# Rotating an 8192 x 8192 matrix: the first macro tile's outputs, TensorE's eight reduced to two

## The chip, the cores and the metric

The kernel runs on one core of one Trainium2 chip. The metric is device time in microseconds (us) of one execution; three runs of the kernel before gave 1258.72, 1258.84 and 1259.64 us, median 1258.84.

A core has several engines that run their own instruction streams: TensorE (PE in the profile), VectorE (DVE), ScalarE (ACT), GpSimd (POOL) and SyncE (SP). SP and ACT also start the DMAs, the transfers between HBM and the on-chip memory (SBUF), each into a queue of its own; 16 DMA engines serve both queues. PSUM is TensorE's output memory.

## The reference

```python
def setup_inputs():
    return {"x": np.random.randn(8192, 8192).astype(np.float32), "k": 1}

def reference(x, k):
    return np.rot90(x, k)
```

With k = 1 the output is `out[8191 - c, r] = x[r, c]`: a transpose with the column order reversed. 268 MB are read and 268 MB are written; there is no arithmetic.

## The kernel before

**Tiles.** The input is cut into 16 macro tiles of 1024 rows x 4096 columns, `kk` = 0 to 15. A macro tile is loaded in eight row blocks (`t` = 0 to 7) of 128 rows x 4096 columns, 2 MB each; load `m = 8 kk + t`. It gives eight outputs (`j` = 0 to 7), each 512 output rows x 1024 output columns, 2 MB; output `n = 8 kk + j`. An output needs its 512-column part, a chunk, of all eight loads. So store `n` can only start when the macro tile's last load has landed.

**Buffers.** Five buffers of 16 KB per partition: two for landing loads, three for outputs. During the first macro tile all five land loads (`load_buf`: loads 0 to 4 go to buffers 0 to 4, loads 5 to 7 to 0 to 2, load 8 to 4, later ones alternate between 0 and 1). Output buffers are given by `START` in macro tile 0 (buffers 3, 2, 4, 3, 2, 4, 3, 2) and by `TURN` later. `room_for` waits until the buffer's last store has landed or, for a buffer's first output, until its last load has been taken out. Between the landing buffers and the outputs lies `ring`, with 63 slots of one chunk. Load `m` writes its chunks into the slots that output `n = m - 8` has just emptied (`slot` runs the other way round in every second macro tile). VectorE therefore turns load `m` only after output `m - 8` has been read out of the ring.

**Two ways to make an output.** `by_pe(kk)` lists the outputs of a macro tile that TensorE makes. For those, VectorE copies the chunk into the ring with its columns reversed, TensorE transposes its 128 x 128 blocks into two PSUM halves, and ScalarE copies the halves to the output buffer (three copies for an output). All others are marked `moved`. For these VectorE writes the chunk with a 32 x 32 block transpose (`STREAM_TRANSPOSE`), and the 32 x 32 blocks are then brought to their places by 16 copies of 32 partitions x 1024 elements: the first 3 by VectorE, the next 8 by GpSimd, the last 5 by ScalarE (`BY_DVE`, `BY_POOL`). In the middle macro tiles `BY_PE = [0, 4]`. Before the change macro tile 0 makes all eight outputs by TensorE, and so does the last one.

The last load of a macro tile has no slot for its last chunk (63 slots for 64 chunks): VectorE reverses that chunk inside the landing buffer, and TensorE transposes it, the "corner", into PSUM. The corner comes ahead of the last part of output 0 on TensorE.

**Order of the work.** Every engine follows a written-out order, with semaphore waits between engines:

- VectorE (`by_vector`) goes through the loads. For load `m`, with `n = m - 8`: if output `n` is moved, it makes its three copies for it; then it waits for the landing, then for GpSimd's and its own copies of output `n` (`s_pool`, `s_dve`), or for TensorE's transposes of it (`s_half`), and then turns the load.
- GpSimd (`by_gpsimd`) goes through the moved outputs: `room_for`, the load that completes the output, seven copies, a wait for ScalarE's copies (`s_act`), the eighth.
- TensorE (`by_tensor`) goes through the outputs of `by_pe`.
- ScalarE (`by_scalar`) issues loads 1, 3 and 5 and half of loads 6 to 9, then goes through all outputs: its five copies, or the three PSUM evictions, then the store's DMA. Ahead of the store of a moved output it waits until VectorE has turned the first chunk of load `n + 8`, which tells it that VectorE's and GpSimd's copies are done.
- SyncE (`by_sync`) issues the other loads, each when its landing buffer has been taken out.

VectorE's and TensorE's programs for macro tiles 2 to 13 and GpSimd's for 1 to 12 run in a hardware loop; the rest is written out.

All operations are issued by one helper, L104 of the profile, so the groups are told apart by engine and tile. L391 is the DMA of `load`.

Of the kernel before, what the change touches and what calls it, by code (L numbers as in the profile page):

```python
# [173 lines left out]
def kernel(tc: tile.TileContext, x: bass.AP, k: bass.AP, out: bass.AP):  # L174
# [7 lines left out]
    KK = len(macros)  # L182
# [11 lines left out]
    outs = [(*o, [(j, g * P) for j in reversed(o[2]) for g in range(G)]) for o in outs]  # L194

    def by_pe(kk):
        if kk in (0, KK - 1):
            return list(range(J))
        return BY_PE if kk < KK - 2 else [*range(0, J, 2), J - 1]

    def in_quadrants(kk, j):
        return j not in by_pe(kk)
# [127 lines left out]
    for m in range(n_load):  # L330
        kk, t = divmod(m, T)
        here = by_pe(kk)
        rest = [j for j in range(J) if j not in here]
        if kk == KK - 1:
            got = [here] if t < T - 1 else [here[:wide], here[wide:-1], here[-1:]]
        elif t < T - 1:
            got = [here, rest]
        else:
            inner = [j for j in here if 0 < j < J - 1]
            got = [here[:1], [j for j in rest if j < J - 1], [J - 1], inner]  # L340
        got = [part for js in got for part in split(js)]
        pieces[m] = got
        for js in got:
            done += 1
            for j in js:
                rev[m, j] = done
# [289 lines left out]
```

## Time and profile before

| | before |
|---|---|
| median of three runs | 1258.84 us |
| the profiled execution, its own time | 1259.08 us |
| its span, first to last instruction | 1257.8 us |
| mean DMA rate over the span | 427 GB/s |
| DVE busy | 793.8 us (63%) |
| POOL busy | 744.0 us (59%) |
| ACT busy | 599.6 us (48%) |
| PE busy | 302.9 us (24%) |

A page of the profile is read from the top: the busy time of each engine, the same in 40 slices of the span (31.4 us each) with the rate of the DMAs beneath, the DMA queues, the chain of work that ended last, and the groups of instructions. A group's line gives engine, operation, what is written and read, shape and count; then the busy time and mean of one; then the idle time of the engine ahead of them and what ended it. A line of the timeline begins with its start and the time it covers, both in us from the span's start; "x3" are three instructions merged, and the bracket is the idle time ahead and what ended it.

### The profile page before, as it was taken

The page shows a single profiled execution, that of the slowest core. Times are in us where ns is not written, and L with a number is a line of the kernel's source. Part 1 is how long each engine was busy: PE and PEld are TensorE (multiplying, and loading weights), DVE is VectorE, ACT ScalarE, POOL GpSimd, SP SyncE. Part 2 cuts the span into 40 slices and gives each one's busy share as a digit, 9 for nine tenths or more (in the row PEclk, how much of TensorE's full clock was granted, in tenths as well). Part 3 has the DMA queues.
Part 4 walks back from the last instruction along what each step waited for, and adds up shares of the span by engine and source line. Part 5 has one row for each costly group of instructions (what it writes and reads, how often), then busy time and mean ns, then how long its engine had stood idle before and what let it go on. Part 6 is the DMA issues. An engine that isn't in the chain of part 4 may idle for free.

```text
span 1257.8 us, 6012 instructions
## 1 busy us (share of the span) xinstructions
PE 302.9 (24%) x1556; PEld 264.8 (21%) x1556; DVE 793.8 (63%) x535; ACT 599.6 (48%) x556; POOL 744.0 (59%) x654
## 2 busy tenths in 40 slices
PE   1555013130131301313022130221302213024273
PEld 0454012130121301212012120121202212024273
DVE  2544866668666676666867667676677766764410
ACT  0334364463644636446364453645535455355364
POOL 0001966668666686666956668576685766965500
PEclk9987556555555555555556555565555556555597
DMA  9999999999999999999999999999999999999999
GB/s 400 420 430 429 429 429 429 429 431 430 430 430 429 430 428 430 428 430 430 430 430 429 431 428 431 428 430 428 430 430 429 430 429 431 427 423 428 427 428 381
DMA packets 36946, 537.09 MB, mean 427 GB/s; under 512 B 4160, under 2 KB 4160, under 8 KB 4160
## 3 DMA queue, kind: packets, MB, share of 16 engines
q10 hardware_dynamic: 19184, 278.93, 52.2%
q1 hardware_dynamic: 17744, 257.96, 48.0%
q8 instruction: 7, 0.11, 0.0%
q14 instruction: 11, 0.09, 0.0%
HBM read 268.44 MB, written 268.44 MB: 427 GB/s over the span
## 4 chain that ended last, share of the span: by engine, by line
DMA 71%; DVE 14%; ACT 4%; POOL 4%; issue 3%; PE 2%; ACTq 0%; DVEq 0%; SPq 0%; POOLq 0%
DMA buf<-in_x_dram 57%; DMA out_dram<-buf 14%; DVE ring L104 14%; ACT buf L104 4%; POOL buf L104 4%; PE ps L104 2%; ACTq L104 0%; DVE buf L104 0%; DVEq L101 0%; SPq L391 0%; DVEq L145 0%; POOLq L101 0%; SPq L311 0%; POOLq L151 0%; SPq L419 0%
## 5 line engine op out<-in xcount | busy, mean ns | idle before, releaser
L104 POOL COPY buf<-ring 32x1024 f32<-32x1024 f32 (+1 forms) x648 | 743.3, 1147 | 440.4 <-DMA out_dram<-buf 244.2
L104 ACT COPY buf<-ring 32x1024 f32<-32x1024 f32 (+1 forms) x405 | 414.8, 1024 | 324.2 <-DVE ring L104 292.5
L104 PE MATMUL ps<-head,ring 128*128 128x128 f32 x1496 | 290.7, 372 | 889.4 <-ACT buf L104 535.8
L104 PEld LDWEIGHTS ps<-head,ring 128*128 128x128 f32 x1496 | 255.3, 197 | 921.5 <-ACT buf L104 548.7
L104 DVE COPY ring<-buf 128x1024 f32<-128x1024 f32 (+5 forms) x152 | 157.7, 1044 | 415.6 <-DMA buf<-in_x_dram 320.1
L104 DVE STREAM_TRANSPOSE ring<-buf 128x3072 f32<-128x3072 f32 (+2 forms) x125 | 358.0, 2872 | 0.0
L104 ACT COPY buf<-ps 128x2048 f32<-128x2048 f32 (+4 forms) x149 | 183.3, 1278 | 313.6 <-DMA out_dram<-buf 149.3
L104 DVE COPY buf<-ring 32x1024 f32<-32x1024 f32 (+1 forms) x243 | 289.5, 1192 | 2.2
L104 PE MATMUL ps<-head,buf 128*128 128x128 f32 x60 | 15.2, 401 | 46.3 <-DVE buf L104 46.3
L104 PEld LDWEIGHTS ps<-head,buf 128*128 128x128 f32 x60 | 9.7, 199 | 52.0 <-issue 44.6
L104 DVE COPY buf<-buf 128x512 f32<-128x512 f32 x15 | 5.8, 387 | 0.0
L104 ACT ACT_TABLE_LOAD x1 | 1.3, 1283 | 3.4 <-PEq L419 3.4
L104 POOL MEMSET head<- 128x128 f32 x1 | 0.2, 204 | 2.9 <-POOLq L419 2.9
L104 POOL TENSOR_SCALAR_AFFINE_SELECT head<-head 128x128 f32<-128x128 f32 x1 | 0.3, 293 | 0.2 <-POOL head L104 0.2
L617 POOL MEMSET const-float32-0.0<- 128x1 f32 x1 | 0.1, 98 | 0.2 <-issue 0.2
L104 ACT COPY head<-head 128x1 f32<-128x1 f32 x1 | 0.2, 191 | 0.0
L617 POOL MEMSET const-bfloat16-1.0<- 128x1 bf16 x1 | 0.1, 100 | 0.0
L617 POOL MEMSET const-uint8-127<- 128x1 uint8 x1 | 0.1, 100 | 0.0
L617 POOL MEMSET const-float32-1.0<- 128x1 f32 x1 | 0.1, 98 | 0.0
## 6 DMA issues: line engine op xcount, KB each, us to landing
out_dram<-buf ACTq DMA_DIRECT2D x128, 2048.0 KB, 15.8
buf<-in_x_dram SPq DMA_DIRECT2D x121, 2048.0 KB, 15.0
buf<-in_x_dram ACTq DMA_DIRECT2D x3, 2048.0 KB, 16.9
buf<-in_x_dram SPq DMA_DIRECT2D x4, 1024.0 KB, 16.1
buf<-in_x_dram ACTq DMA_DIRECT2D x4, 1024.0 KB, 16.4
```

Source lines behind the costliest of these rows:

```text
L104: i = getattr(e, self.name)(*self.args, **kwargs)
L617: nc = _bacc.Bacc("TRN2", target_bir_lowering=False, num_devices=1)
```

## The change

In macro tile 0 TensorE makes outputs 0 and 4, as in the middle macro tiles. Outputs 1, 2, 3, 5, 6 and 7 are moved.

```diff
     def by_pe(kk):
-        if kk in (0, KK - 1):
+        if kk == KK - 1:
             return list(range(J))
         return BY_PE if kk < KK - 2 else [*range(0, J, 2), J - 1]
```

`by_pe` is read wherever a program is written: by `moved`, by the pieces in which VectorE turns a load, and by the loops of all engines over the outputs. So for loads 0 to 7 VectorE copies two chunks of eight and transposes six. While it turns loads 8 to 15 it adds three copies for each of six outputs. GpSimd gets eight copies for each of six outputs, and ScalarE five copies in the place of three evictions. TensorE keeps the two outputs and the corner. Buffers, DMAs and their order on each queue are as before.

## The prediction

> **What bounds the kernel now.** I read the page's slices first, then the chain, then the groups, then the timeline of the first 154 us, where the change lies.
>
> ```profile
> DMA  9999999999999999999999999999999999999999
> GB/s 400 420 430 429 429 429 429 429 431 430 430 430 429 430 428 430 428 430 430 430 430 429 431 428 431 428 430 428 430 430 429 430 429 431 427 423 428 427 428 381
> ...
> DMA 71%; DVE 14%; ACT 4%; POOL 4%; issue 3%; PE 2%; ACTq 0%; DVEq 0%; SPq 0%; POOLq 0%
> ```
>
> The DMA engines are busy in every slice, at some 430 GB/s: one 2 MB transfer (2.097 MB) takes 4.88 us of all 16 engines. No engine is above 63%. Engine work costs nothing by itself; it costs only when both DMA queues run dry. So the question is whether the change opens a gap in the transfers, and the place is the start, where the first store needs eight loads. Slice 0 holds the start-up, slice 1 a dip that I return to. The timeline of the start:
>
> ```profile
> 32.60 4.50 DVE L104 COPY ring<-buf 128x4096 f32<-128x4096 f32 x2 [5.26 <-DMA buf<-in_x_dram]
> ...
> 42.31 0.43 DVE L104 COPY ring<-buf 128x512 f32<-128x512 f32 x1 [2.56 <-DMA buf<-in_x_dram]
> 42.77 0.43 DVE L104 COPY buf<-buf 128x512 f32<-128x512 f32 x1
> ...
> 45.87 0.64 ACTq L104 DMA_DIRECT2D out_dram<-buf  x1
> ...
> 53.27 0.58 ACTq L104 DMA_DIRECT2D out_dram<-buf  x1
> ...
> 59.03 0.55 ACTq L104 DMA_DIRECT2D out_dram<-buf  x1
> ```
>
> Loads 4 and 5 land together at 32.6, load 7 at 42.3; the corner is ready at 43.2 and store 0 is issued at 45.87, 2.66 later. Stores 1 and 2 follow before store 0 is through, so that the store queue is two deep from here on. What a moved output costs is seen where macro tile 1 begins:
>
> ```profile
> 122.42 1.53 DVE L104 COPY ring<-buf 128x1024 f32<-128x1024 f32 x1 [5.97 <-DMA buf<-in_x_dram]
> 123.88 3.36 DVE L104 STREAM_TRANSPOSE ring<-buf 128x3072 f32<-128x3072 f32 x1
> 127.17 4.33 DVE L104 COPY buf<-ring 32x1024 f32<-32x1024 f32 x3
> 132.43 0.69 DVE L104 COPY ring<-buf 128x1024 f32<-128x1024 f32 x1 [0.93 <-POOL buf L104]
> ...
> 133.16 0.55 ACTq L104 DMA_DIRECT2D out_dram<-buf  x1
> 133.75 5.25 ACT L104 COPY buf<-ring 32x1024 f32<-32x1024 f32 x5 [6.35 <-DVE ring L104]
> 136.34 4.34 DVE L104 COPY buf<-ring 32x1024 f32<-32x1024 f32 x3
> 142.68 0.69 DVE L104 COPY ring<-buf 128x1024 f32<-128x1024 f32 x1 [2.00 <-POOL buf L104]
> ...
> 143.40 0.55 ACTq L104 DMA_DIRECT2D out_dram<-buf  x1
> ```
>
> VectorE waits for POOL ahead of each turn, and stores come every 10.25 us (133.16, 143.40, 153.65). A load and a store take the DMA 2 x 4.88 = 9.76 us. Three moved outputs in a row are thus 0.5 us each slower than the DMA; macro tile 1 lives off the stores queued before it. In macro tile 0 nothing is queued yet.
>
> **The change part by part.**
>
> *Turning loads 0 to 7.* Removed: copies of 128x4096, 2.29 us a load. Added: a 128x1024 copy and a 128x3072 transpose; from 132.43 to 136.34 that is 3.91 us. Loads land every 4.88 us, but loads 0 to 5 in pairs, so VectorE falls behind: load 4 from 32.6, 5 from 36.5, 6 from 40.4, 7 from 44.3 (landed 42.3). In macro tile 1's last load the corner was ready 3.55 us after the first chunk was begun (112.57 to 116.12). So the corner is at 47.85, not 43.2. Loads 8 to 10 need loads 4 to 6 turned, by 44.3 at the latest; the loads ahead of them run until about 52. Hidden; uncovered, it would cost the 4.65 us.
>
> *Store 0.* Corner + 2.66 = 50.5, 4.6 us later. Load 9 runs to 52.2 and load 10 is behind it on SP's queue, so nothing idles. Load 10 and store 0 are through at 52.2 + 9.76 = 62.0 (packet records of before: 62.2 and 62.8); I take 62.2. ScalarE's first eviction also starts some 3 us later, because it issues half of load 9 first, which needs load 5; its cover is the corner.
>
> *Output 1 to 3.* Removed: TensorE's 32 transposes and ScalarE's 3.9 us of evictions each, both off the path. Added on ScalarE: 5.25 us, begun as soon as the store before is issued, 5 us before POOL needs it. Added on VectorE: 4.34 us, inside POOL's time. Added on POOL: 8 copies, 10.2 us. POOL can begin when the corner is transposed (buffer 2): 47.85 + 1.1 (four of the eight transposes that took 1.98 us) + 0.1 = 49.1. Done at 59.3. Queued behind it are VectorE's turn of load 9 and, by the first chunk of that, store 1, 0.7 us later: 60.0 against 53.27. Then every 10.25 us: store 2 at 70.3, store 3 at 80.5. Load 11 (after load 9 turned) goes out at 63.3, load 12 at 73.5, load 13 at 83.8.
>
> *Do both queues run dry?* That hangs on the time from issue to flow, call it d. At 62.2 only store 1 is there, from 60.0 + d; it and load 11 are 9.76 us of work, then store 2 is needed, and so on. With no gap, store 3 is needed at 62.2 + 2 x 9.76 = 81.7; it flows from 80.5 + d. Loss: d - 1.2, spread over three places near 62, 72 and 82. Bounds for d: the first transfers were issued at 0.91, and by 4.0 the window 2 to 4 us had moved 656 KB, 1.5 us of full rate, so they flowed from 2.5: d = 1.5 (nothing else running). At the other end, a load issued at 168.27 had its first packet at 171.75, its queue empty since 170.5: d = 3.5 (other queue full). In between, the store issued at 1094.06 had its first packet at 1096.20 behind a running store: 2.1. I take 2.1, nearest to store 1's case: loss 0.9 us. With 1.5: 0.3. With 3.5: 2.3.
>
> The Trainium skill ("DMA: Bandwidth & Descriptors", Specifications) puts the first byte of such a transfer at about 0.6 us. By that the loss would be nothing; the trace's 1.5 to 3.5 disagree.
>
> To this come the edges, where 16 DMA engines do not stop and start together. The one change from loads to stores that before shows is this dip:
>
> ```profile
> 50.00:52.00 2.00, 1.35 (x12) 1.00 (x10) 1.20 (x1) 2.00 (x2) 0.00 (x0) 1.00 1.02 311
> 52.00:54.00 2.00, 0.82 (x8) 0.70 (x7) 1.21 (x2) 1.24 (x2) 0.00 (x0) 1.00 1.09 467
> ```
>
> The last column is GB/s: a mean of 389 over 4 us, 0.4 us lost. I charge 0.4 at two of the three places (0.8), bounds none and three (1.2).
>
> *Output 4 by TensorE.* ScalarE is free of output 3 at 81; 3.9 us of evictions give store 4 at 85. Load 13 (83.8) and it flow by 87.3 even with d = 3.5; store 3 alone runs to 82.6 + 4.9 = 87.5. Then load 13, store 4 and load 14 (88) are 14.6 us of work, to 102; store 5 goes out with load 13's turn, at about 97. From here the queues cover each other, as in the middle macro tiles, whose slices stay at 428 to 431. TensorE's remaining work and outputs 5 to 7 cost nothing: six outputs of 10.2 us are 61 us of POOL in eight pairs' 78.
>
> POOL's 10.25 has bounds too. Its eight copies took 9.29 us for macro tile 2's first moved output (from 199.82) and 11.02 in macro tile 14 (1070.12 to 1081.13), where VectorE copies larger pieces beside them. The first gives no loss; the second, at 11.08 a period, makes store 3 2.5 us later (three periods 0.83 longer). I take 10.25: same instructions, same neighbours.
>
> Sum: 0.9 + 0.8 = 1.7 us. The profiled execution took 1259.08 (span 1257.8 and 1.3 around it); 1260.8 for its like. It stands 0.24 above the median, so 1260.5. A measurement here tells 0.2%, 2.5 us, from no change: from 1256.3 to 1261.4 is the same.
>
> **The rivals.**
>
> *Slower: the handover is long.* Place: stores 1 to 3. It decides from d = 2.9 (d - 1.2 + 0.8 = 2.5). For it: the load with 3.5, and POOL's 11.02. Against: store 1 is issued behind a store that still runs. With both ends, 2.3 + 2.5 + 1.2 = 6.0: 1264.8.
>
> *No loss.* d at or under 1.5, or POOL nearer to 9.3. For it: the first transfers. Against: 10.25 came three times. Time 1258.8 to 1259.1. The first byte of the Trainium skill's page above would make this the case.
>
> *Faster.* The dip at 50 could close, as store 0 and load 10 no longer begin together: -0.4, 1258.4, inside the same. I see nothing that gives 2.5; every later slice is full already.
>
> **How the numbers follow.** Chances: short gaps as forecast 0.46 (0.42 of it inside 0.2%), long handover 0.34, no loss 0.16, something faster 0.04 (no mechanism found, kept for what the rows do not show). Same 0.42 + 0.16 = 0.58; slower 0.34 + 0.04 = 0.38; faster 0.04. Range: from the no-loss case less the runs' 0.1 and the dip's 0.4, 1258.4, to the long handover, 1264.8.
>
> **What would show it.** Store issues at 50.5, 60.0, 70.3, 80.5, 85; POOL's first copy at 49.1; the DMA rate under 430 only in short windows near 62, 72 and 82, and full after 90. Wrong if store 1 is before 58 or after 62, if three stores are not 10.25 apart, if the DMA loses time after 90 or inside 10 to 50, or if a rate below 420 stays without both queues being empty.

## The result, and the profile after

The changed kernel takes 1260.89 us (median of 19 runs, 1259.83 to 1262.06) against 1258.90 for the kernel before (19 runs beside them, 1258.47 to 1259.64): 2.0 us more, ratio 1.0014, 95% interval 1.0008 to 1.002. That is inside the 0.2% that I called the same, at its slow end; a ratio of 1, no change at all, lies just outside the interval. The profiled execution took 1260.89, its span is 1259.5 us.

The page's slices of the kernel after:

```profile
DMA  9999999999999999999999999999999999999999
GB/s 399 417 399 430 431 428 430 430 429 430 428 430 430 429 430 429 430 429 429 430 430 429 431 428 432 430 428 430 430 430 431 427 431 430 429 427 430 428 425 381
...
L104 POOL COPY buf<-ring 32x1024 f32<-32x1024 f32 (+1 forms) x696 | 785.7, 1129 | 399.8 <-ACT buf L104 196.9
```

The DMA row is full as before. The rate tells more: the third slice (63.0 to 94.5 us) has 399 GB/s where before had 430, and the others are within 4 of before. GpSimd's 48 copies more are there and cost nothing in the other slices.

The same place in windows; a line gives the window, its length, the busy time of PE, PEld, DVE, ACT and POOL (with counts), TensorE's clock, the share of time that the DMA engines are busy, and GB/s. The kernel before:

```profile
50.00:60.00 10.00, 6.35 (x51) 5.40 (x50) 5.18 (x3) 6.94 (x6) 0.00 (x0) 0.98 1.01 408
60.00:70.00 10.00, 6.93 (x40) 6.30 (x39) 3.98 (x2) 3.79 (x3) 0.00 (x0) 0.68 1.00 429
70.00:80.00 10.00, 5.79 (x36) 5.26 (x34) 3.98 (x2) 3.79 (x3) 0.00 (x0) 0.83 1.01 431
80.00:90.00 10.00, 5.57 (x34) 4.75 (x32) 3.98 (x2) 3.79 (x3) 0.00 (x0) 0.83 1.01 433
90.00:100.00 10.00, 6.31 (x30) 5.17 (x30) 3.98 (x2) 3.80 (x3) 0.00 (x0) 0.68 0.99 421
100.00:120.00 20.00, 11.07 (x62) 9.59 (x62) 7.87 (x7) 7.65 (x7) 0.00 (x0) 0.76 1.01 431
...
1100.00:1200.00 100.00, 34.72 (x156) 30.18 (x157) 50.74 (x38) 49.82 (x48) 54.01 (x42) 0.54 1.01 426
```

The kernel after:

```profile
50.00:60.00 10.00, 3.46 (x15) 3.06 (x15) 8.99 (x6) 5.63 (x6) 9.65 (x9) 0.89 1.01 397
60.00:70.00 10.00, 1.65 (x8) 1.66 (x9) 8.99 (x6) 5.21 (x5) 9.65 (x9) 0.50 0.98 382
70.00:80.00 10.00, 1.38 (x7) 0.98 (x5) 8.99 (x6) 5.20 (x5) 9.65 (x9) 0.67 1.01 419
80.00:90.00 10.00, 4.51 (x19) 3.78 (x19) 9.51 (x6) 7.80 (x7) 7.31 (x7) 0.58 1.01 404
90.00:100.00 10.00, 0.00 (x0) 0.00 (x0) 2.95 (x4) 1.26 (x3) 8.51 (x8) 0.59 1.00 413
100.00:120.00 20.00, 3.34 (x15) 2.94 (x16) 16.46 (x14) 12.84 (x13) 9.83 (x10) 0.50 1.01 430
...
1100.00:1200.00 100.00, 32.80 (x146) 28.28 (x147) 50.06 (x37) 50.37 (x47) 55.97 (x44) 0.53 1.01 428
```

From 50 to 100 us the five windows lie 11, 47, 12, 29 and 8 GB/s lower: 107 GB/s over 10 us is 1.07 MB, or 2.5 us at 430. After 100 the rate is as before. Between 1100 and 1200 the kernel after moves 2 GB/s more, 0.2 MB or 0.5 us. That leaves 2.0, near the 1.8 us by which the two profiled executions differ (1260.89 and 1259.08).

POOL is at 9.65 of 10 us from 50 to 80. What it sets is seen in the timeline of the kernel after, whose columns are those of before:

```profile
47.39 0.38 DVE L104 COPY buf<-buf 128x512 f32<-128x512 f32 x1
...
49.09 38.46 POOL L104 COPY buf<-ring 32x1024 f32<-32x1024 f32 x31 [44.96 <-PE ps L104]
...
50.45 0.64 ACTq L104 DMA_DIRECT2D out_dram<-buf  x1
...
59.21 1.56 DVE L104 COPY ring<-buf 128x1024 f32<-128x1024 f32 x1 [0.98 <-POOL buf L104]
...
60.80 0.58 ACTq L104 DMA_DIRECT2D out_dram<-buf  x1
...
70.88 0.55 ACTq L104 DMA_DIRECT2D out_dram<-buf  x1
...
80.96 0.55 ACTq L104 DMA_DIRECT2D out_dram<-buf  x1
...
85.28 0.55 ACTq L104 DMA_DIRECT2D out_dram<-buf  x1
```

The corner is ready at 47.8, POOL begins at 49.09, and stores 1, 2 and 3 are issued 10.08 us apart, each behind a VectorE copy that waited for POOL.

### The profile page after: what moved, and what is told of

Read it like the earlier page. It is cut to its first block, busy times and chain, and to the rows that moved or that the text cites. A ratio compares the mean times of both kernels' runs of the same rounds, so it can differ in the third digit from the quotient of the medians.

```text
span 1259.5 us, 5714 instructions
## 1 busy us (share of the span) xinstructions
PE 274.7 (22%) x1368; PEld 239.6 (19%) x1368; DVE 808.7 (64%) x562; ACT 608.1 (48%) x568; POOL 786.4 (62%) x702
## 4 chain that ended last, share of the span: by engine, by line
DMA 69%; DVE 17%; POOL 5%; issue 3%; ACT 3%; PE 2%; ACTq 0%; DVEq 0%; SPq 0%; POOLq 0%
DMA buf<-in_x_dram 64%; DVE ring L104 17%; DMA out_dram<-buf 5%; POOL buf L104 5%; ACT buf L104 3%; PE ps L104 2%; ACTq L104 0%; DVE buf L104 0%; DVEq L101 0%; SPq L391 0%; DVEq L145 0%; SPq L311 0%; SPq L419 0%; ACTq L101 0%; POOLq L101 0%
## 5 line engine op out<-in xcount | busy, mean ns | idle before, releaser
L104 POOL COPY buf<-ring 32x1024 f32<-32x1024 f32 (+1 forms) x696 | 785.7, 1129 | 399.8 <-ACT buf L104 196.9
L104 ACT COPY buf<-ring 32x1024 f32<-32x1024 f32 (+1 forms) x435 | 445.5, 1024 | 352.7 <-DVE ring L104 326.3
L104 PE MATMUL ps<-head,ring 128*128 128x128 f32 x1308 | 261.6, 379 | 908.6 <-ACT buf L104 533.4
L104 DVE COPY ring<-buf 128x1024 f32<-128x1024 f32 (+5 forms) x152 | 152.8, 1010 | 402.9 <-DMA buf<-in_x_dram 349.9
L104 PEld LDWEIGHTS ps<-head,ring 128*128 128x128 f32 x1308 | 229.4, 201 | 937.5 <-ACT buf L104 541.5
L104 DVE STREAM_TRANSPOSE ring<-buf 128x3072 f32<-128x3072 f32 (+1 forms) x134 | 384.2, 2875 | 0.0
L104 ACT COPY buf<-ps 128x2048 f32<-128x2048 f32 (+3 forms) x131 | 161.1, 1278 | 279.1 <-DMA out_dram<-buf 136.4
L104 DVE COPY buf<-ring 32x1024 f32<-32x1024 f32 (+1 forms) x261 | 284.5, 1090 | 2.4
```

The lines of the kernel that those rows point to most:

```text
L104: i = getattr(e, self.name)(*self.args, **kwargs)
```

## The experiments

Three theories. A: while outputs 1 to 3 are made, 10 us each, nothing is queued, and the DMA waits for what follows on them. B: VectorE turns loads 0 to 7 more slowly, and the corner is late. C: the loss belongs to outputs 5 to 7, or to the way macro tile 1 is entered.

### Outputs 1 to 3 back to TensorE; outputs 5 to 7 back to TensorE

The first kernel:

```diff
+        if kk == 0:
+            return [0, 1, 2, 3, 4]
```

> Macro tile 0: TensorE makes outputs 0 to 4, outputs 5, 6 and 7 are moved. Theory A (the pace of outputs 1 to 3: with a 10.1 us period for each they hold up loads 11 to 13 and store 4 while nothing is queued): stores 1 and 2 come some 6 us apart, the store queue is two deep before the first moved output, the loss is gone, 1258.9 us give or take 0.4. Theory C (the loss belongs to outputs 5 to 7 or to the way macro tile 1 is entered): it stays, 1260.9. Theory B (VectorE turns loads 0 to 7 more slowly and the corner comes late): the turn is 3.1 us instead of 3.9 and the corner about 1 us late of 4.65, so about 0.4 is left, 1259.3.

Measured: 1259.22 us (11 runs), ratio to before 1.0002, interval 0.9993 to 1.0011. The second kernel has `[0, 4, 5, 6, 7]` there.

> Macro tile 0: TensorE makes outputs 0, 4, 5, 6 and 7, outputs 1, 2 and 3 are moved. Theory A: the loss is that of the changed kernel, 1260.9 us (+2.0), less some 0.8 as the corner comes earlier (the turn of a load is 3.1 us). Theory C: no loss, 1258.9. Theory B: 1259.3.

Measured: 1260.79 us (11 runs), ratio 1.0015, interval 1.0006 to 1.0024. So the loss goes with outputs 1 to 3, and C falls. The first kernel also speaks against B: its store 0 is issued at 50.32, as late as the changed kernel's 50.45, and VectorE turns a load in 4.39 us where the changed kernel needs 3.86, with no loss. My expectation had its corner only 1 us late; that was wrong. Its stores then come 6 to 7 us apart:

```profile
50.32 0.65 ACTq L104 DMA_DIRECT2D out_dram<-buf  x1
...
57.50 0.58 ACTq L104 DMA_DIRECT2D out_dram<-buf  x1
...
63.26 0.55 ACTq L104 DMA_DIRECT2D out_dram<-buf  x1
```

For the second kernel I had taken off 0.8 us because its corner comes earlier. Its store 0 does come 0.9 us earlier than the changed kernel's, but its time is only 0.1 us less. Its stores stand at the 10 us pace:

```profile
49.59 0.64 ACTq L104 DMA_DIRECT2D out_dram<-buf  x1
...
60.34 0.58 ACTq L104 DMA_DIRECT2D out_dram<-buf  x1
...
70.42 0.55 ACTq L104 DMA_DIRECT2D out_dram<-buf  x1
```

### The slow turn alone

The kernel before, with VectorE's copies of loads 0 to 7 cut into short pieces and the corner last:

```diff
+            if kk == 0:
+                got = [here[:1], inner, [J - 1]]
...
+                if kk == 0:
+                    for j in js:
+                        for lo in (0, CH // 2):
+                            ...  # one copy of 128x256
```

> The kernel before (TensorE makes all of macro tile 0), but VectorE copies loads 0 to 7 in 16 pieces of 128x256, about 0.26 us each and so 4.2 us a load instead of 2.29, and the corner comes last: at about 48.5 us instead of 43.2, as in the changed kernel. Theory B (the late corner and the slow turn): the loss is there, 1260.9 us. Theory A: store 0 is issued 5 us later, but stores 1 and 2 follow 6 us apart, and the time is that of before, 1258.9 us give or take 0.4.

Measured: 1259.11 us (11 runs), ratio 1.0001, interval 0.9992 to 1.001. The pieces were shorter than I had reckoned, 0.20 us each, so the corner came at 46.15 and store 0 at 48.83 instead of 45.87: 3.0 us late of the changed kernel's 4.6.

```profile
48.83 0.64 ACTq L104 DMA_DIRECT2D out_dram<-buf  x1
...
55.96 0.58 ACTq L104 DMA_DIRECT2D out_dram<-buf  x1
...
61.71 0.55 ACTq L104 DMA_DIRECT2D out_dram<-buf  x1
```

Those 3 us cost nothing; with the run above, where all 4.5 us cost nothing, B falls too.

### The pace, made slower

Outputs 1 to 3 with more copies on GpSimd and fewer on ScalarE:

```diff
+    def pool_takes(n):
+        return BY_POOL + 2 if n < 4 else BY_POOL
```

> The changed kernel, but for outputs 1, 2 and 3 GpSimd makes 10 and ScalarE 3 of the copies, instead of 8 and 5: each output takes about 2.3 us longer. Theory A: nothing covers it any more, so the three periods add 6.9 us: 1267.8 us, and the DMA rate shows it between 60 and 95 us. Theories B and C: 1260.9.

Measured: 1268.01 us (4 runs), ratio 1.0072, interval 1.0056 to 1.0087. With `BY_POOL + 1`:

> The changed kernel, but for outputs 1, 2 and 3 GpSimd makes 9 and ScalarE 4 of the copies: half the step of the run with ten, whose time was 1268.0. If every microsecond of the period counts three times, it lies midway between the changed kernel's 1260.9 and 1268.0: 1264.4 us. If there were a step, such as a missed handover, it would be near one of the two.

Measured: 1264.70 us (4 runs), ratio 1.0042, interval 1.0026 to 1.0058. The kernel with ten copies, its stores 1 to 3 and one of its windows:

```profile
62.98 0.58 ACTq L104 DMA_DIRECT2D out_dram<-buf  x1
...
75.21 0.55 ACTq L104 DMA_DIRECT2D out_dram<-buf  x1
...
87.44 0.55 ACTq L104 DMA_DIRECT2D out_dram<-buf  x1
```

```profile
60.00:70.00 10.00, 0.00 (x0) 0.00 (x0) 8.59 (x5) 3.12 (x3) 9.61 (x10) 0.50 0.75 285
```

Store 3 is issued 6.5 us later than in the changed kernel (87.44 - 80.96), and the kernel takes 7.1 us longer. With nine copies store 3 is at 84.26, 3.3 us later, and the time is 3.8 us longer. From the changed kernel on, every microsecond by which store 3 comes later is paid in full, and somewhat over.

### The pace, made faster

```diff
+    def pool_takes(n):
+        return BY_POOL - 1 if n < J else BY_POOL
```

> The changed kernel, but in macro tile 0 GpSimd makes 7 and ScalarE 6 of a moved output's 16 copies, instead of 8 and 5. Stores 1, 2 and 3 should come 8.9 us apart instead of 10.1, under the 9.76 us that a load and a store take the DMA. Theory A: load 13 is issued some 3 us earlier, the loss is 0 to 0.3, 1258.9 to 1259.2 us. Theories B and C: unchanged, 1260.9.

Measured: 1260.26 us (11 runs), ratio 1.0013, interval 1.0004 to 1.0022. My expectation failed. The stores (60.41, 70.10, 78.90) show why: the first two are 9.69 us apart, not 8.9. GpSimd's last copy waits for ScalarE's six, which ScalarE begins only when it has issued the store before:

```profile
57.70 8.23 POOL L104 COPY buf<-ring 32x1024 f32<-32x1024 f32 x7 [1.33 <-ACT buf L104]
...
67.39 1.03 POOL L104 COPY buf<-ring 32x1024 f32<-32x1024 f32 x1 [1.46 <-ACT buf L104]
```

A pace of 9.69 is no better than the DMA's 9.76; only the third interval, 8.80, gains on it. The median is 0.6 us under the changed kernel's, which the scatter of the runs (1259.30 to 1262.82) does not tell from nothing. To shorten ScalarE's wait, the store's condition was changed first by itself:

```diff
-                e.wait_ge(s_rev, rev[n + T, pieces[n + T][0][0]])
+                if n < J:
+                    e.wait_ge(s_pool, moved_until(n))
+                    e.wait_ge(s_dve, moved_until(n))
+                else:
+                    e.wait_ge(s_rev, rev[n + T, pieces[n + T][0][0]])
```

> The changed kernel, but in macro tile 0 ScalarE issues the store of a moved output when GpSimd's and VectorE's copies are done, and not when VectorE has turned the first chunk of the load behind it. Stores 1 to 3 go out about 1.6 us earlier, the loads do not. If the gaps are where the prediction put them, at late stores, about 1 us of the loss goes: 1259.9 us. If it is the loads behind them that flow late (3.5 us from issue), the stores only end earlier and the wait for the load grows by as much: within 0.3 of the changed kernel, 1260.9.

Measured: 1260.66 us (11 runs, 1258.87 to 1262.62), ratio 1.0016, interval 1.0007 to 1.0025. The stores did go out 1.6 us earlier (59.23, 69.31, 79.40) with load 11 in its place, and the median is 0.2 us under the changed kernel's. By the time alone that is nearer to late loads than to late stores. The trace does not bear it out. In the profiled execution loads 11 to 13 did not keep their 3.5 us: their first packets came 2.06 to 2.52 us after issue. Up to 100 us it is only some 0.6 us behind the kernel before, and another 0.8 goes from 100 to 120 (413 GB/s against 431), behind outputs 1 to 3. But the runs are spread over 3.8 us, and this execution (1259.81) is one of the shorter ones. Alone it doesn't settle where the gaps are. Then both edits together:

> The two edits of the run with GpSimd 7 and ScalarE 6 and of the run with early stores together. In the first of them stores stayed 9.69 us apart, because GpSimd's last copy waited 1.4 us for ScalarE, which starts its copies only behind the store; with the early store ScalarE starts 1.6 us sooner, so the period should be about 8.5 us. Theory A (pace): now that three outputs are really faster than 3 x 9.76, loads 12 and 13 come 2 and 3 us earlier than in that run and only the handover around store 1 (near 67 us, at most 0.5 us) is left: 1258.9 to 1259.5 us. If the loss hangs on something else than the pace, as that run's 1260.26 could be read: 1260.3 to 1260.7.

Measured: 1259.21 us (11 runs, 1258.22 to 1262.68), ratio 1.0004, interval 0.9995 to 1.0013.

```profile
58.58 0.58 ACTq L104 DMA_DIRECT2D out_dram<-buf  x1
...
67.82 0.55 ACTq L104 DMA_DIRECT2D out_dram<-buf  x1
...
76.81 0.55 ACTq L104 DMA_DIRECT2D out_dram<-buf  x1
```

The pace is 9.1 us (I had said 8.5), under 9.76, and 1.7 of the 2.0 us are gone. TensorE still makes two outputs only, VectorE still turns the loads slowly: the timing of outputs 1 to 3 is enough to explain most of the loss. The run has the earlier stores as well as the faster pace (store 1 goes out at 58.58, 2.2 us earlier), so it does not say what each is worth.

### The corner first

```diff
+            if kk == 0:
+                got = [here[:1], [J - 1], [j for j in rest if j < J - 1], inner]
```

> The changed kernel, but in load 7 VectorE reverses the corner right behind the first chunk, ahead of the transposes. The corner is ready at about 45.1 us instead of 47.8, store 0 goes out near 47.8, and GpSimd begins when the load is turned, at 48.2 instead of 49.1. Theory A: stores 1 to 3 and load 13 come 0.9 us earlier, the loss shrinks by as much, 1260.0 us. Theory B (the corner itself): most of the loss goes, 1259.3. Theory C: 1260.9.

Measured: 1259.96 us (11 runs), ratio 1.0009, interval 1.0 to 1.0018. The corner came at 45.2, store 0 at 47.91, POOL's first copy at 48.42 and store 1 at 60.15, 0.65 earlier; the time is 0.9 us shorter. It is as A expected, a shift of the whole row that is worth about itself. The kernel in which only outputs 1 to 3 are moved does not confirm that last part: its store 1 is 0.46 us earlier than the changed kernel's, and its time only 0.1 us shorter.

### A try at the dip near 50 us

The kernel before, with load 10 on both queues:

```diff
-EARLY = range(T + 2)
-BOTH = EARLY[-4:]
+EARLY = range(T + 3)
+BOTH = EARLY[-5:]
```

> The kernel before, but load 10 is issued in halves on both queues too, as loads 6 to 9 are. It asks whether the dip at 50 to 52 us, which every run so far has, comes from load 10 being alone on SP's queue when store 0 begins behind load 9. If so, the dip of about 0.8 us goes: 1258.1 us. If not: 1258.9, or later by up to 0.5, as store 0 begins behind half of load 10.

Measured: 1258.57 us (11 runs), ratio 0.9998, interval 0.9989 to 1.0007. The window from 50 to 52 us now moves 451 GB/s instead of 311, but the dip has only moved: from 54 to 58 us it moves 377 and 336 GB/s, where the kernel before has 401 and 426. So the time is not measurably less. What makes the dip was not followed further, and no version measurably beat the kernel before.

## Why the prediction was right, step by step

**The outcome.** 1260.5 was forecast, no change that 0.2% can tell, in a range from 1258.4 to 1264.8; 1260.89 was measured. The likeliest case came: short gaps while outputs 1 to 3 are made. The run with nine copies, whose stores 1 to 3 are 11.16 us apart, shows what the period of 11.08 at the slow end of the long-handover rival would have cost: it takes 1264.70, and the rival came to 1264.8 with d at 3.5 besides. Two of my signs came out otherwise. The dips lie near 67, 77 and 87, not near 62, 72 and 82, and a little is still lost after 90 (413 GB/s against 421), where I had nothing. The dip at 50, which the faster rival would have closed, moved to 52 to 56 (369 and 328 GB/s).

**Times of the steps.** Forecast and measured: corner 47.85 and 47.8; POOL's first copy 49.1 and 49.09; store 0 at 50.5 and 50.45; store 1 at 60.0 and 60.80; store 2 at 70.3 and 70.88; store 3 at 80.5 and 80.96; store 4 at 85 and 85.28. The pace was 10.08 instead of 10.25, an interval that the lines of the kernel before show twice and not three times. Store 1 is 0.8 late because VectorE's copy of the first chunk took 1.56 us, not 0.69: POOL had begun its next copy at 59.18 and VectorE began at 59.21. The Trainium skill ("SBUF — State Buffer", SBUF: two separate sides) says that VectorE, in its two-port modes, and GpSimd share a pair of ports which one of them locks for a whole instruction. The records agree in that both slow down: beside each other VectorE's 32x1024 copies take 1.43 to 1.45 us instead of 0.68, and POOL's 1.40 instead of 1.03. That is less than the 1.71 that one after the other would take, so the whole instruction is not seen to be locked.

**The loss, by its terms.** I had d - 1.2 = 0.9 for late stores and 0.8 for edges, 1.7 in all; 2.5 us went missing up to 100 us, and 2.0 in the median. With the measured times the form for late stores gives 80.96 + 1.67 - 81.7 = 0.9 again, for two reasons that cancel. By the packet records the stores flowed sooner after their issue than I took: 1.25, 1.63 and 1.67 us, not 2.1. The times put store 3 0.5 us later. That this term came out is luck, for it stood for gaps ahead of the stores. Stores 2 and 3 had their first packets, at 72.52 and 82.64, while a load still ran (to 73.34 and 83.12), and there the kernel after loses nothing.

**The step that failed** is the one on load 13: "Load 13 (83.8) and it flow by 87.3 even with d = 3.5; store 3 alone runs to 82.6 + 4.9 = 87.5." I let only stores be late, and kept the loads behind them safe by a margin of 0.2 us. Even by its own figures that held for load 13 alone: store 4, issued at 85, flows at 88.5 with d = 3.5. For load 13 the margin wasn't there either. Load 13 was issued at 84.24, its first packet is at 87.81; store 4's is at 89.88, where I had them both by 87.3. Store 3 ended at 88.21. From 62.2, where load 10 and store 0 were through as forecast, the five transfers up to store 3 are 24.4 us of work, to 86.6: 1.6 us were lost in that stretch. About 0.3 had gone before it, and the rest followed until load 13 and store 4 ran together. The rate of the kernel after shows two of the places, in windows of 2 us:

```profile
66.00:68.00 2.00, 0.00 (x0) 0.00 (x0) 1.99 (x2) 0.66 (x1) 1.92 (x3) 0.50 0.94 270
86.00:88.00 2.00, 2.00 (x11) 2.00 (x11) 2.00 (x1) 1.98 (x3) 1.51 (x2) 0.50 0.88 303
```

At 67.65 load 11 has its first packet, and store 1 its last at 67.94; at 87.81 and 88.21 it is load 13 and store 3. I had looked for gaps near 62, 72 and 82, ahead of the stores; the deep ones are where a store runs out and the next load only begins. The packet records give the sizes, when the bytes moved up to each time are compared with those of the kernel before. The kernel after falls back by 0.75 us from 66 to 68, by 0.3 from 76 to 78 and by 0.9 from 86 to 95, where loads 11, 12 and 13 (with store 4) join; from 70 to 74 and from 80 to 84, where stores 2 and 3 join, it falls back by no more than 0.03. The edges that I charged at two places belong here.

**What was costed at nothing** did cost nothing: the slower turn and the 4.6 us on store 0 (shown by the kernel with outputs 0 to 4 on TensorE, whose store 0 is as late), outputs 5 to 7, and what TensorE and ScalarE were spared.

**What stays open.** The gaps lie at the loads, but that does not say what faster loads alone would win: behind a pace of 10 us the next store could then be the one that is missed. No run moved the loads alone. It is also open why loads 11 to 13 flowed sooner in the run with early stores, and why the runs of the changed kernel scatter more than those before, over 2.2 us against 1.2.

## What to carry to other kernels

Where the DMA is the bound, compare the pace of an engine chain with the time of the transfers it feeds (here 10.1 against 9.76 us), and ask how many transfers are queued ahead when it begins. The same 10 us pace cost nothing in macro tile 1, behind a queue two deep; at the start, with nothing queued, what was added to it was paid microsecond by microsecond. Count the handover in both directions, the next load's as well as the next store's.

## What I had not expected of the hardware

A transfer that joins while another runs alone on the DMA engines can get in late. By the packet records of the kernel after, loads 11, 12 and 13 were issued 3.9 to 4.0 us before the end of a store that ran alone; their first packets came 3.58, 3.39 and 3.57 us after issue, 0.3 to 0.7 us before that end. Stores 1 to 3 were issued 1.4 to 2.5 us before the end of the transfer then running and had theirs after 1.25 to 1.67 us. In the kernel with ten copies, whose stores 1 to 3 were issued when nothing or almost nothing ran, the stores needed 1.21 to 1.24 us, and the loads behind them again 3.50 to 3.61. It is not a fixed delay, though: in the profiled execution with early stores the same loads, issued 2.7 to 3.8 us before a store's end, needed only 2.06 to 2.52. Store 0, issued just before load 10 began, needed 4.45 us, although its own queue was empty from 50.97 on. No run tested this by itself.
